# Second expert pass: the loads of activations and tables cut into pieces of two and four blocks

## Chip, cores and metric

The kernel runs on one core of a Trainium2 chip. The metric is device time in microseconds (us), the median over several executions.

## What is computed

The program is a first transformer block (windowed attention beside a state-space mixer, then an expert layer) followed by a second block of two layers. The change is in the expert layer of the first block, which is this part of the reference:

```
def peer_ffn(h, w_query, sub_keys, peer_u, peer_v):
    ...
        q = (hc @ w_query).astype(jnp.float32).reshape(PEER_CHUNK, PEER_HEADS, PEER_DK)
        ...
        v1, i1 = lax.top_k(s1, PEER_TOPK)
        v2, i2 = lax.top_k(s2, PEER_TOPK)
        ...
        sc, ci = lax.top_k(cand, PEER_TOPK)
        idx = ...
        g = jax.nn.softmax(sc, axis=-1)
        u_sel = peer_u[idx]
        act = jax.nn.gelu(jnp.einsum('chkd,cd->chk', u_sel, hc)...) * g
        v_sel = peer_v[idx]
        return jnp.einsum('chk,chkd->cd', act.astype(hc.dtype), v_sel)
```

Each of 512 tokens picks 8 x 16 of 16384 single-neuron experts. An expert's activation is the gelu of the token's dot product with a row of `peer_u`, times a gate; the output is the sum of the chosen rows of `peer_v` by these weights.

## The kernel before, in words

For three of the four groups of 128 tokens (384 tokens, `SD` = 384) the layer is computed densely. The 16384 experts lie in 128 blocks of 128. The text speaks of "expert n" for block n of the first pass and of "block n" for block n of the second.

- **First pass** (`experts_in`, driven by `phase_p1`): for each n a 512 KB tile `wraw` of `peer_u` is loaded by SyncE (SP), split by `split_sb` into a high part `whi` (ScalarE, ACT, L276) and a low part `wlo` (VectorE, DVE, L277), and multiplied by TensorE (PE) in 24 matmuls `pl` of 128x384 (L282 and L284 use `whi` and `wlo` of the weight). The gelu of the result goes to DRAM as `adram`, 12 KB of 8 blocks side by side in each partition.
- **Routing** (`route`): top-k, softmax and one-hot products that build the gate table `gdram`. Its DVE instructions (MATCH_REPLACE, MAX, MAX_INDEX, `cand`, `O`) are handed out between the experts of the first pass.
- **Sparse remainder** (`sparse_experts`): the fourth group of 128 tokens is done by gathering rows (GpSimd, POOL, L1133, with the index copy L1131 on DVE), dots on DVE in the first pass (L1142) and weighted sums `sacc` on DVE in the second (L1155).
- **Second pass** (`phase_p2`, 128 blocks): `fetch_ag(g)` loads for eight blocks the activations A (L1355, 1536 KB) and the gates G (L1356, 1536 KB) on SP's queue. `prep(n)` multiplies A by G for block n (L1376, DVE) and splits it into `ahl`: the high part on ACT (L276), the low part on DVE (L277). Then 18 matmuls `acc` of 128x512 use `ahl` and the split tile `whi`, `wlo` of a 512 KB `wraw` of `peer_v`.

Buffers: `wraw`, `whi`, `wlo` and `ahl` have three each, A and G two each. So `ahl` of block n+2 needs PE to have finished block n-1, the load of A for group g+1 needs the last `ahl` of group g-1, and the load of G for group g+2 needs the last multiply of group g. Every engine and every queue works in order. The order on each engine is set by a scheduler that runs the program against a simulated timeline when the kernel is built, so a change of a few DMAs can reorder other instructions. Program text:

```
if n % 8 == 0 and n < 120:
    self.fetch_ag(n // 8 + 1)
if n + 1 < 128:
    prep(n + 1)
ws.append((n, self.W.next(held=0)) + act.pop(n))
```

Of the kernel before, what the change touches and what calls it, by code (L numbers as in the profile page):

```python
# [204 lines left out]
class Stream:  # L205
# [46 lines left out]
    def next(self, held=0):  # L252

        n = self.n_used
        self._split(n + 1 + self.ahead - held)
        self.n_used += 1
        return self.got.pop(n)


class Kernel:  # L260
# [810 lines left out]
    def phase_p1(self):  # L1071
        nc, pp = self.nc, self.pp

        ring = self.p0.tile([128, 4, D], F32, name="ring", tag="xres")
        more = pp.tile([128, 2, D], F32, name="ring2")
        self.ring = [ring[:, j] for j in range(4)] + [more[:, j] for j in range(2)]
        self.sums = []
        self.hs = pp.tile([128, D], F32, name="hs")
        nc.gpsimd.dma_start(out=self.hs, in_=self.hdram)

        self.iota2 = pp.tile([128, 128, 2], F16, name="iota2")
        nc.vector.tensor_copy(self.iota2, self.iota[:, :, None].to_broadcast([128, 128, 2]))
        self.iota16 = pp.tile([128, 16, 16], BF16, name="iota16")
        nc.vector.tensor_copy(self.iota16, self.iota[:, :16, None].to_broadcast([128, 16, 16]))
        self.query()
        self.AG = {}
        first, rest, dense = self.route(0), chain(*(self.route(t) for t in range(1, TT))), self.experts_in()
        self.sparse = self.sparse_experts()

        have = 0.0  # L1090
        left = True
        for n, _ in enumerate(dense):
            have += 3.5
            while have > 0 and (d := next(first, None)) is not None:
                have -= d
            if have > 0:
                if n >= 12:
                    self.some(1.15)
                have -= 1.6
                while have > 0 and left:  # L1100
                    d = next(rest, None)
                    left = d is not None
                    have -= d or 0.0
                have = min(have, 0.0)
            if n >= 114 and not left and not self.AG:
                self.fetch_ag(0)
        for _ in chain(first, rest):
            pass

# [237 lines left out]
    def fetch_ag(self, g):  # L1347

        nc, pp = self.nc, self.pp
        A = pp.tile([128, 8 * SD + 16], F32, name="A2", tag="A2", bufs=2)  # L1350
        if g:
            self.hold = self.places(A, 8 * SD, 16)
        A = A[:, :8 * SD].rearrange("p (j t) -> p j t", j=8)
        G = pp.tile([128, SD // 32, 8, 32], F32, name="G2", tag="Gst", bufs=2)
        nc.sync.dma_start(out=A, in_=self.adram[g])  # L1355
        nc.sync.dma_start(out=G, in_=self.gdram[:, :, g * 8:g * 8 + 8].rearrange("t p i k -> p t i k"))  # L1356
        self.AG[g] = (A, G)

    def phase_p2(self):

        nc, pp = self.nc, self.pp
# [22 lines left out]

        if not self.AG:
            self.fetch_ag(0)
        prep(0)
        for n in range(128):
            if n % 8 == 0 and n < 120:
                self.fetch_ag(n // 8 + 1)  # L1390
            if n + 1 < 128:
                prep(n + 1)
            ws.append((n, self.W.next(held=0)) + act.pop(n))
            if n < 116:
                self.some(1.0)
            elif n == 116:
                for _ in self.sparse:
                    pass

                self.xres = self.p0.tile([128, TT, D], F32, name="xres")  # L1400
                nc.sync.dma_start(out=self.xres, in_=self.xdram)
            elif n == 120:
                x = self.xres[:, 0]
                v.tensor_tensor(x, x, self.sacc, op=OP.add)
                norm(0, None)
            if 128 - self.LAST <= n < 127:
                continue
            for t in range(1, TT):
                ts = slice((t - 1) * 128, t * 128)
                for m, w, hi, lo in ws:  # L1410
                    for h in range(2):
                        hs = slice(h * 512, h * 512 + 512)
                        self.mm3(acc[t][h], (hi[:, ts], lo[:, ts]), (w[0][:, hs], w[1][:, hs]), m == 0, m == 127)
                if n == 127:
                    for h in range(2):
                        x = self.xres[:, t, h * 512:h * 512 + 512]
                        v.tensor_tensor(x, x, acc[t][h], op=OP.add)
                        st = self.ln_stats(pp, self.xres[:, t], h, st if h else None)
                    norm(t, st)
            ws = []  # L1420
# [625 lines left out]
```

## Time and profile before

| | |
|---|---|
| median of 3 runs | 3328.93 us (3325.83 to 3332.78) |
| the profiled execution | 3332.02 us, span 3330.2 us, mean granted TensorE clock 0.983 |
| PE busy | 3169.8 us, 95% of the span |
| DVE busy | 2327.8 us, 70% |
| ACT busy | 1411.0 us, 42% |
| POOL busy | 909.1 us, 27% |
| first pass with routing | about 455 to 1152 us |
| second pass | about 1152 to 1705 us |

A row of the waits names an engine and line, what it waited for, the total, the count and the longest. A row of the timeline has start, duration, engine, line, operation, output, inputs, shapes; in brackets stands the idle time just before it and what ended it. PEclk is the granted TensorE clock as a share of full speed.

### The profile page before, as it was taken

To read this page: it belongs to the slowest core of one execution; us is meant where nothing else is said; L and a number is where in the kernel's file an instruction comes from. 1 tells how busy PE (TensorE), PEld (TensorE's weight loads), DVE (VectorE), ACT (ScalarE), POOL (GpSimd) and SP (SyncE) were. 2 spreads that over 40 slices of the span, in tenths; PEclk is the share of its full clock that TensorE was granted. 3 is DMA by queue.
4 is the path that set the end of the run, shared out by engine and by line. 5 is a ranking of instruction groups with operands and counts; after the bars stand their busy time and mean duration, and the time that the engine had idled before them with its cause. 6 is when DMAs were issued, how large, how long until landed. Compare 5 with 4: busy or idle time off the path is not lost.

```text
span 3330.2 us, 46422 instructions
## 1 busy us (share of the span) xinstructions
PE 3169.8 (95%) x17023; PEld 2704.6 (81%) x17023; DVE 2327.8 (70%) x4748; ACT 1411.0 (42%) x2396; POOL 909.1 (27%) x1114
## 2 busy tenths in 40 slices
PE   6888899999999899999999999999999999999997
PEld 5776689999999778777888778888888877888886
DVE  8899479999888678777867845555437774555534
ACT  4345434456555233333335733344314662434421
POOL 4342010333233323232222652311002365031101
PEclk9999899999999899999999999999999999999999
DMA  3464233889999989899742122222224112222222
GB/s 128 123 151 130 69 118 117 331 321 344 367 342 332 361 308 352 321 343 344 286 161 64 45 89 76 84 96 99 97 95 134 43 46 84 96 90 99 95 95 70
DMA packets 176164, 578.19 MB, mean 174 GB/s; under 512 B 19120, under 2 KB 52912, under 8 KB 169920
## 3 DMA queue, kind: packets, MB, share of 16 engines
q1 hardware_dynamic: 114576, 352.37, 30.8%
q0 software_dynamic: 43056, 165.69, 14.1%
q10 hardware_dynamic: 18304, 57.15, 4.4%
q8 instruction: 134, 2.20, 0.3%
q14 instruction: 94, 0.77, 0.1%
HBM read 511.72 MB, written 63.44 MB: 173 GB/s over the span
## 4 chain that ended last, share of the span: by engine, by line
PE 69%; DVE 14%; DMA 8%; issue 3%; POOL 3%; ACT 2%; SPq 0%; DVEq 0%; ACTq 0%; POOLq 0%
PE pl L284 11%; PE pl L282 11%; PE pl L283 11%; DMA wraw<-in_peer_v 4%; PE mm L282 2%; PE acc L282 2%; PE mm L283 2%; PE mm L284 2%; PE acc L284 2%; PE acc L283 2%; DMA A<-adram 2%; DVE wlo L277 2%; PE T L283 2%; PE T L284 2%; PE T L282 2%
## 5 line engine op out<-in xcount | busy, mean ns | idle before, releaser
L277 DVE TENSOR_TENSOR wlo<-wraw,whi 128x1024 fp32r<-128x1024 f32 x476 | 587.0, 1234 | 516.2 <-ACT whi L276 502.5
L276 ACT CAST whi<-wraw 128x1024 fp32r<-128x1024 f32 x507 | 529.4, 1048 | 807.7 <-PE pl L283 348.7
L282 PE MATMUL pl<-hhi,whi 128*128 128x384 f32 (+1 forms) x1128 | 390.1, 346 | 10.1 <-ACT whi L276 10.1
L284 PE MATMUL pl<-hhi,wlo 128*128 128x384 f32 (+1 forms) x1128 | 387.0, 345 | 10.2 <-DVE wlo L277 6.0
L283 PE MATMUL pl<-hlo,whi 128*128 128x384 f32 (+1 forms) x1128 | 388.3, 344 | 0.0
L282 PE MATMUL pl<-xThi,whi 128*128 128x512 f32 x944 | 370.4, 392 | 0.0
L284 PE MATMUL pl<-xThi,wlo 128*128 128x512 f32 x944 | 368.9, 391 | 0.0
L283 PE MATMUL pl<-xTlo,whi 128*128 128x512 f32 x944 | 368.3, 390 | 0.0
L283 PE MATMUL acc<-wlo,ahl 128*128 128x512 f32 x744 | 290.7, 394 | 0.0
L284 PE MATMUL acc<-whi,ahl 128*128 128x512 f32 x744 | 290.4, 393 | 0.0
L1133 POOL DMA_INDIRECT ring<-in_peer_v,A x128 | 160.1, 1251 | 382.2 <-DVE A L1131 276.9
L1133 POOL DMA_INDIRECT ring<-in_peer_r,A x123 | 158.3, 1287 | 329.6 <-DVE A L1131 304.1
L282 PE MATMUL acc<-whi,ahl 128*128 128x512 f32 x744 | 226.0, 396 | 10.5 <-ACT whi L276 10.5
L284 PEld LDWEIGHTS pl<-hhi,wlo 128*128 128x128 f32 x1128 | 213.3, 189 | 17.1 <-DVE wlo L277 13.1
L282 PEld LDWEIGHTS pl<-hhi,whi 128*128 128x128 f32 x1128 | 213.8, 190 | 15.3 <-ACT whi L276 11.3
L283 PEld LDWEIGHTS pl<-hlo,whi 128*128 128x128 f32 x1128 | 213.8, 190 | 3.7
L284 PEld LDWEIGHTS pl<-xThi,wlo 128*128 128x128 f32 x944 | 177.3, 188 | 39.2 <-issue 0.5
L283 PEld LDWEIGHTS pl<-xTlo,whi 128*128 128x128 f32 x944 | 177.2, 188 | 38.7 <-issue 1.0
L282 PEld LDWEIGHTS pl<-xThi,whi 128*128 128x128 f32 x944 | 177.3, 188 | 36.4 <-issue 0.5
L282 PEld LDWEIGHTS acc<-whi,ahl 128*128 128x128 f32 x744 | 139.1, 188 | 46.5 <-ACT whi L276 15.0
L2027 POOL TENSOR_TENSOR cv<-cv 128x512 f32<-128x512 f32 x44 | 57.0, 1296 | 431.0 <-ACT cv L2026 431.0
L283 PEld LDWEIGHTS acc<-wlo,ahl 128*128 128x128 f32 x744 | 139.9, 188 | 32.5
(715 smaller groups left out, 7349.4 us busy)
## 6 DMA issues: line engine op xcount, KB each, us to landing
wraw<-in_peer_u SPq DMA_DIRECT2D x128, 512.0 KB, 6.2
wraw<-in_peer_v SPq DMA_DIRECT2D x128, 512.0 KB, 8.4
wraw<-in_up SPq DMA_DIRECT2D x88, 512.0 KB, 3.4
adram<-A ACTq DMA_DIRECT2D x64, 384.0 KB, 6.7
A<-adram SPq DMA_DIRECT2D x16, 1536.0 KB, 7.4
gdram<-G ACTq DMA_DIRECT2D x12, 2048.0 KB, 10.8
G<-gdram SPq DMA_DIRECT2D x16, 1536.0 KB, 14.5
wraw<-in_down SPq DMA_DIRECT2D x44, 512.0 KB, 3.4
```

Of the source, the lines that this page charges most:

```text
L276: self.nc.scalar.copy(hi, src)
L277: (eng or self.nc.vector).tensor_tensor(lo, src, hi.bitcast(F32), op=OP.subtract)
L282: mm(out, l[0], r[0], start=start, stop=False)
L283: mm(out, l[0], r[1], start=False, stop=False)
L284: mm(out, l[1], r[0], start=False, stop=stop)
L1133: nc.gpsimd.indirect_dma_start(out=self.ring[n % R], out_offset=None, in_=src[n // 128], in_offset=bass.IndirectOffsetOnAxis(ap=ix, axis=0))
L2027: nc.gpsimd.tensor_tensor(ts[0], ts[0], ts[1], op=OP.mult)
```

## The change

`fetch_ag` becomes the start of a generator. A is loaded in four pieces of two blocks (384 KB, 128x768), G in two pieces of four blocks (768 KB, 128x12x128, where a contiguous run in DRAM is 512 bytes and was 1 KB). The first pieces are issued by the call, the others by `next` at every second block, and in the first pass at every further expert. The number of DMAs on SP's queue grows by four for each of 16 groups.

```diff
             if n >= 114 and not left and not self.AG:
                 self.fetch_ag(0)
+            if self.AG:
+                next(self.ag, None)
...
-        nc.sync.dma_start(out=A, in_=self.adram[g])
-        nc.sync.dma_start(out=G, in_=self.gdram[:, :, g * 8:g * 8 + 8].rearrange("t p i k -> p t i k"))
         self.AG[g] = (A, G)
+
+        def fetch():
+            for j in range(0, 8, 2):
+                nc.sync.dma_start(out=A[:, j:j + 2], in_=self.adram[g, :, j:j + 2])
+                if j % 4 == 0:
+                    nc.sync.dma_start(out=G[:, :, j:j + 4], in_=self.gdram[:, :, g * 8 + j:g * 8 + j + 4].rearrange("t p i k -> p t i k"))
+                yield
+        self.ag = fetch()
+        next(self.ag)
...
         if not self.AG:
             self.fetch_ag(0)
+        for _ in self.ag:
+            pass
         prep(0)
         for n in range(128):
             if n % 8 == 0 and n < 120:
                 self.fetch_ag(n // 8 + 1)
+            elif n % 2 == 0:
+                next(self.ag, None)
```

In the changed file the lines move: A is L1361, G L1363, the multiply L1385, the routing lines and `sparse_experts` stand two lines further down.

Three places show what the scheduler makes of it.

SP's queue in the second pass, from the load of A for blocks 48 to 55 (`A2_13140` before, `A2_13164` now) to the load of G for blocks 64 to 71. Before (`wraw` of blocks 41 to 43, G, then `wraw` of blocks 44 and 45):

```order
L1355 DMA A2_13140<-adram_84 128x3072
L226 DMA wraw_13024<-in_peer_v 128x1024
L226 DMA wraw_13055<-in_peer_v 128x1024
L226 DMA wraw_13086<-in_peer_v 128x1024
L1356 DMA G2_13645<-gdram_81 128x12x256
L226 DMA wraw_13117<-in_peer_v 128x1024
L226 DMA wraw_13152<-in_peer_v 128x1024
```

Now (one `wraw`, of block 41, between the third and the fourth piece, those of blocks 42 to 44 ahead of G, and block 45 behind it):

```order
L1361 DMA A2_13164<-adram_84 128x768 x3
L226 DMA wraw_13047<-in_peer_v 128x1024
L1361 DMA A2_13164<-adram_84 128x768
L226 DMA wraw_13078<-in_peer_v 128x1024
L226 DMA wraw_13110<-in_peer_v 128x1024
L226 DMA wraw_13141<-in_peer_v 128x1024
L1363 DMA G2_13677<-gdram_81 128x12x128 x2
L226 DMA wraw_13176<-in_peer_v 128x1024
L226 DMA wraw_13207<-in_peer_v 128x1024
```

The pieces are not spread over the eight blocks: three or four pieces of A stand in a row, both halves of G in a row, since a tile's first piece needs the whole buffer free. In the change as a whole, the first wraw behind G is that of blocks 21, 27, 37, 45, 51, 61, 69, 75, 85, 93 and 99 instead of 20, 29, 36, 44, 52 and so on, every eighth. A for blocks 32 to 39 stands ahead of the wraw of block 24, G behind that of block 26.

ACT in the second pass at blocks 43 to 48. Before, beginning with `ahl` of block 45, then `whi` of 44:

```order
L276 CAST ahl_13268<-A2_12888 128x384
L276 CAST whi_13210<-wraw_13117 128x1024
L276 CAST ahl_13299<-A2_12888 128x384
L276 CAST whi_13241<-wraw_13152 128x1024
L276 CAST ahl_13330<-A2_12888 128x384
L276 CAST whi_13272<-wraw_13183 128x1024
L276 CAST whi_13303<-wraw_13214 128x1024
```

Now, beginning with `ahl` of block 45 and `whi` of 44 as well (`ahl_13326` is block 46, `ahl_13358` block 47, `whi_13266` block 45):

```order
L276 CAST ahl_13295<-A2_12908 128x384
L276 CAST whi_13235<-wraw_13141 128x1024
L276 CAST ahl_13326<-A2_12908 128x384
L276 CAST ahl_13358<-A2_12908 128x384
L276 CAST whi_13266<-wraw_13176 128x1024
L276 CAST whi_13299<-wraw_13207 128x1024
L276 CAST whi_13330<-wraw_13239 128x1024
```

Before, `whi` of block n stands behind `ahl` of n+1; now, here, `ahl` of block 47 stands ahead of `whi` of block 45. Over the whole pass `ahl` of n+2 stands ahead of `whi` of n before at blocks 4, 20 and 116, and now at blocks 4, 21, 27, 45, 51, 69, 75, 93, 99 and 116. DVE has the low parts in the same order.

DVE in the first pass, the last rows ahead of `wlo` of expert 28 (`wlo_6496`). Before:

```order
L1131 COPY A_6648<-sidx_5519 128x1
L1142 ISA ring_4239,A_6648<-ring_4239,hs_4241 128x1024
L1142 ISA A_6648 128x1
L1327 TENSOR_TENSOR O_6164<-iota2_4243,T3_6050 128x1024
L277 TENSOR_TENSOR wlo_6496<-wraw_6321,whi_6495 128x1024
```

Now:

```order
L1133 COPY A_6648<-sidx_5519 128x1
L1144 ISA ring_4239,A_6648<-ring_4239,hs_4241 128x1024
L1144 ISA A_6648 128x1
L1248 MAX sc_9281<-cand_9274 128x8
L1334 TENSOR_TENSOR O_6164<-O_6164,g3_6051 128x2x256 x2
L1334 TENSOR_TENSOR O_6180<-O_6180,g3_6051 128x2x256 x2
L277 TENSOR_TENSOR wlo_6496<-wraw_6321,whi_6495 128x1024
```

Before, four rows stand between `wlo` of expert 27 and the first of these (a MAX and, for the other dot, an index copy and two ISA rows). Now 19 rows stand there: those four, both `O` builds (L1329 now), four `cand` rows and nine rows of small instructions. So between the two `wlo` the change has, beyond what stood there before, four `cand`, one `O` build, the four products of `O` (the last two rows ahead of `wlo`, each x2) and 13 small ones (MAX, MAX_INDEX, MATCH_REPLACE, `k`, `r3`). Up to `wlo` of expert 27 the same instructions have been issued in both.

## Rows read from the trace of the kernel before

**Rows 1.** Busy time by stretch: us, PE, PEld, DVE, ACT, POOL, PEclk, DMA share, GB/s.

```profile
600.00:700.00 100.00, 94.81 (x572) 92.35 (x572) 97.57 (x296) 49.59 (x69) 36.73 (x30) 0.98 0.92 334
...
1100.00:1152.00 52.00, 38.49 (x191) 37.04 (x192) 32.61 (x50) 11.17 (x16) 15.07 (x12) 0.84 1.00 365
1152.00:1705.00 553.00, 539.91 (x2335) 435.35 (x2334) 436.51 (x625) 194.70 (x264) 156.20 (x150) 1.00 0.84 312
```

**Rows 2.** What PE waited for, 1150 to 1710 us.

```profile
PE acc L282 <- ACT whi L276: 10.5, 10, 2.0
```

**Rows 3.** The chain of waits, 1430 to 1482 us: start, us, what.

```profile
1449.72 7.30 DMA A<-adram
...
1457.05 2.57 DVE A L1376 x6
...
1462.52 15.05 DMA wraw<-in_peer_v
...
1477.60 1.05 ACT whi L276
```

**Rows 4.** Timeline of PE, second pass: first matmuls after a wait.

```profile
1238.78 0.50 PE L282 MATMUL acc<-whi,ahl 128*128 128x512 f32 x1 [1.55 <-ACT whi L276]
...
1375.67 0.50 PE L282 MATMUL acc<-whi,ahl 128*128 128x512 f32 x1 [2.02 <-ACT whi L276]
...
1478.69 1.65 PE L282 MATMUL acc<-whi,ahl 128*128 128x512 f32 x6 [1.10 <-ACT whi L276]
```

**Rows 5.** Timeline of ACT, blocks 20 to 22 of the second pass.

```profile
1233.08 0.51 ACT L276 CAST ahl<-A 128x384 fp32r<-128x384 f32 x1 [3.60 <-PE acc L284]
1237.27 0.51 ACT L276 CAST ahl<-A 128x384 fp32r<-128x384 f32 x1 [3.68 <-PE acc L284]
1237.69 2.94 ACT L276 CAST whi<-wraw 128x1024 fp32r<-128x1024 f32 x3
```

**Rows 6.** Timeline of DVE and SP's queue, 1440 to 1485 us.

```profile
1457.05 3.84 DVE L1376 TENSOR_TENSOR A<-A,G 128x384 f32<-128x384 f32 x8 [1.64 <-DMA A<-adram]
...
1460.92 0.38 SPq L1356 DMA_DIRECT2D G<-gdram  x1
```

**Rows 7.** Timeline of DVE, experts 27 to 30 of the first pass.

```profile
656.69 1.22 DVE L277 TENSOR_TENSOR wlo<-wraw,whi 128x1024 fp32r<-128x1024 f32 x1
...
660.99 1.21 DVE L277 TENSOR_TENSOR wlo<-wraw,whi 128x1024 fp32r<-128x1024 f32 x1
...
662.33 0.67 DVE L1327 TENSOR_TENSOR O<-iota,T 128x1024 f16<-128x1024 f16 x1
...
662.99 0.75 DVE L1332 TENSOR_TENSOR O<-O,g 128x512 f16<-128x512 f16 x2
...
666.27 0.88 DVE L1234 TENSOR_TENSOR cand<-sall 128x128 f32<-128x128 f32 x4
```

**Rows 8.** Timeline of DVE, small routing instructions near 610 us.

```profile
609.62 0.73 DVE L1246 MAX8 sc<-cand 128x8 f32<-128x64 f32 x5
```

**Rows 9.** Timeline of PE: the first use of `wlo` of expert 28.

```profile
663.68 0.33 PE L284 MATMUL pl<-hhi,wlo 128*128 128x384 f32 x1
```

**Rows 10.** What PE waited for, 560 to 720 us.

```profile
PE pl L284 <- DVE wlo L277: 4.4, 4, 2.3
```

**Rows 11.** What PE waited for, 1080 to 1152 us.

```profile
PE pl L282 <- ACT whi L276: 8.5, 2, 6.4
PE pl L284 <- DVE A L1131: 4.2, 1, 4.2
```

**Rows 12.** Busy time by stretch, at the passage between the passes (columns as rows 1).

```profile
1120.00:1130.00 10.00, 5.80 (x20) 5.80 (x21) 9.10 (x13) 1.25 (x2) 5.24 (x4) 0.54 1.08 360
```

**Rows 13.** The chain of waits, 1086 to 1152 us.

```profile
1093.40 23.16 DMA G<-gdram
...
1117.06 3.37 DVE A L1376 x7
```

**Rows 14.** DMA queues, 1120 to 1126 us (pieces of 1 KB): packets, MB, share of 16 engines.

```profile
q1 hardware_dynamic: 2034, 2.07, 108.2%
```

**Rows 15.** DMA queues, 204 to 208 us (pieces of 512 bytes).

```profile
q10 hardware_dynamic: 272, 0.13, 11.4%
```

**Rows 16.** DMA rate in 40 slices, 1440 to 1475 us.

```profile
GB/s 392 410 407 417 234 28 0 126 403 70 169 403 183 267 323 393 435 370 389 431 407 421 435 393 412 417 407 408 400 389 391 330 284 301 355 391 392 406 398 410
```

## The prediction

> **What bounds the kernel now.** I read the busy times by stretch first. In the second pass (the last row of [rows 1]) PE is busy for 539.91 of 553 us at full granted clock and the DMA engines for 84%; DVE works 436.51 us and ACT 194.70, so both have room on the whole. PE sets the time there, and what a change can win is little: all of PE's waits for `whi` are 10.5 us, ten times [rows 2]. Next comes the chain of waits. One period of it reads [rows 3]: A is issued and lands 7.30 us later, DVE multiplies A by G, then G for a later group is issued [rows 6], the first `wraw` behind it on SP's queue takes 15.05 us, and ACT's `whi` comes only then. PE stands 1.10 us (the last of [rows 4]). Eight blocks, one in each group from block 44 to block 100, show this.
>
> The timeline of ACT shows the other two waits, at blocks 4 and 20 [rows 5]: two `ahl` in a row, each begins only after 3.6 us of waiting for PE, and `whi` comes behind the second at once, three of them in 2.94 us. So `whi` of block 20 was not late by its transfer; it stood behind `ahl` of block 22, which needed PE to have finished block 19. PE then had nothing to do for 1.55 us (the first of [rows 4]). This is a wait that the order alone makes. Taking 1.55 for block 4 as well, the eight others share 10.5 - 3.1 = 7.4 us, 0.93 each.
>
> In the first pass PE is nearly full too, but from 600 to 700 us DVE is busy for 97.57 of 100 us [rows 1], and PE waited four times for a `wlo`, 4.4 us [rows 10]. At the passage between the passes (1100 to 1152 us) PE works only 38.49 of 52 us with the DMA engines full; its waits [rows 11] and a clock of 0.54 between 1120 and 1130 us, the lower level (1.2 GHz) after the stop [rows 12], make up the loss. The chain there is two G loads, 23.16 us, then seven multiplies [rows 13].
>
> **The change, part by part.** It adds 64 DMA issues on SP, moves no byte more, cuts G's runs from 1 KB to 512 bytes, and through the scheduler moves work on ACT, DVE and SP.
>
> *Smaller G pieces.* In a stretch of 1 KB pieces 2034 packets took 108.2% of 16 engines for 6 us [rows 14]: 103.9 engine-us, 51 ns each. For 512 bytes it is 11.4% of 16 engines for 4 us over 272 packets [rows 15], 27 ns. A G load of 1536 packets of 1 KB becomes 3072: 1536 x 51 = 78 engine-us against 3072 x 27 = 83, over 16 engines +0.3 us; if a 512 byte packet cost two thirds of a large one (34 ns), +1.6. I take +0.5 us per G load, in the second pass inside the terms below.
>
> *More issues on SP.* One issue of G takes 0.38 us [rows 6]. Three more A issues delay the `wraw` behind them by about 1.1 us, one more G issue by 0.4. Queued behind are only `wraw` loads; ACT waits for them, and only the first behind G is ever late, so 0.4 us of it count below.
>
> *A forced wait at eight more blocks.* By the order, `whi` of block n now stands behind `ahl` of block n+2 at blocks 21, 27, 45, 51, 69, 75, 93 and 99 (block 4 stays, 20 goes). Nothing that is faster elsewhere can help: `ahl` of n+2 cannot start before PE ends block n-1, and PE has no `whi` for n. Price 1.55 us each, as at block 20: +12.4. The bounds: 0, if ACT reaches them early for a reason that I don't see, and 2.02, the longest wait of the kind with a transfer in it [rows 4].
>
> *The waits of the group go.* Behind G the first `wraw` is now that of 45 or 61 where it was 44 or 60; this gives PE a block, 553/128 = 4.3 us, more than the longest wait there. So -7.4, and -1.55 for block 20. Together the second pass stands at +3.4.
>
> *What is late next.* In every third group (27, 51, 75, 99) the first `wraw` behind G serves a block nearer to the release of A: four blocks after the last `ahl` that A waits for, where it was five. That costs 4.3 us of lead. Given back is this: the multiplies no longer begin when all of A is there; with two left after the last piece instead of eight, 6 x 3.84/8 = 2.9 us [rows 6]. So the `wraw` comes 0.93 + 4.3 - 2.9 + 0.4 (SP) = 2.7 us late where the order costs 1.55 anyway: about +1 each, +4 in all. Bounds: 0 (the order's wait covers it) and +2.9 each, if nothing is given back by the multiplies, +12.
>
> *First pass.* At expert 28 DVE gets to `wlo` later: ahead of it stand, by starts rather than by overlapping durations, four `cand` (0.8 us), one `O` build (0.6) and four products (1.3) [rows 7] and 13 small instructions of at most 0.73/5 = 0.15 [rows 8], 2.0: +4.7 us. In the trace `wlo` ends at 662.2 [rows 7] and PE first uses it at 663.68 [rows 9], 1.5 us later. PE loses 3.2 us. Later DVE has done that routing work already, but PE is full afterwards and cannot win it back. Bounds: 0, if the 1.5 us of slack grow because DVE's own waits for gathers move into the cover; +5, if the stop brings the lower clock again as at the passage.
>
> *The passage.* Two pairs of G loads, +0.5 us each, lie on the chain [rows 13]: +1 for the first pair, +1 for the second; against it, seven multiplies behind the last landing become three or four, -1.7, since half of G lands earlier. I take 0, from -3 (one `sacc` less is on the path too) to +3 (lower clock for longer).
>
> **Sum.** 3.4 + 4 + 3.2 + 0 = +10.6 us on the profiled execution of 3332.02 us: 3342.6. That execution was 3.1 us above the median of the runs shown (3328.93), so I forecast 3339.5 us. A measurement of this kernel tells some 0.2%, 6.7 us, from no change: below 3322.3 is faster, above 3335.6 slower.
>
> **Rivals.**
>
> *Slower by transfers* (0.10): the pieces stand together on SP, the burst of gathers that A releases comes into the smaller G packets, and the `wraw` of blocks 27, 51, 75 and 99 is late by its full 4.3 us: +12 instead of +4 there and +2 at the passage, 3350. For it: 15.05 us for one `wraw` behind G [rows 3]. Against: DVE's multiplies do start earlier.
>
> *No difference* (0.29): the pieces are not spread at all by the order, so the change hardly does what it says; the first pass keeps its slack (0) and the late `wraw` hide in the order's wait (0). Then +3.4 is left: 3332. For it: all terms are small, and DVE has room on the whole.
>
> *Faster, by a lead at the passage and in every group* (0.13): the multiplies run piece by piece, so G and all `wraw` behind it come up to 2.9 us earlier in every group, ACT is never behind, and the order's wait shrinks, because `ahl` of n+2 and `whi` of n both stand ready and only 1.05 us of `whi` [rows 3] is left partly beside PE's last matmuls. With x the order's wait per block and -3 at the passage, the sum is 8x - 8.95 - 3; it is below -6.7 once x is under 0.66 us. With x = 0.3 and no loss in the first pass: 3319. Against it [rows 4]: with three `whi` ready to go, PE still waited 1.55.
>
> *Many DMAs, each with its own start-up* (0.02). The trace shows rates near 400 GB/s while the queue holds only 512 KB loads and gathers [rows 16], so starts lie beside other transfers. If they did not, four more issues in each of 14 groups would lengthen the chain of rows 3 by at least an issue each and in the worst case by the wait of A itself, 7.30 us per group: over 100 us, 3430. Here the Trainium skill speaks against the change: its page "DMA: Bandwidth & Descriptors", in "Anatomy of one DMA", fits 2.0 us of fixed time to each DMA, and in "Rules for kernel authors" asks for at least 1 MiB per DMA; by it four more DMAs would be 8 us a group, +112 us as an estimate. That fit is for DMAs issued from GpSimd, these are issued from SP, and the 400 GB/s with 512 KB loads do not bear it out as a cost in series.
>
> **Chances.** The forecast itself, +7 to +15 us, has 0.46. Slower by over 0.2%: 0.46 + 0.10 + 0.02 = 0.58; within 0.2%: 0.29; faster: 0.13. The range reaches from the rival on the other side with x = 0.3 (3319, rounded to 3320) to the transfers' case with the first pass at its upper bound (3352); some 0.05 lie below and some 0.08 above.
>
> **What would show it.** Right: in the waits of the second pass, PE behind `whi` some nine or ten times for 17 to 20 us instead of 10.5, at the nine blocks named, ACT with two `ahl` before that `whi`, and no wait at 44, 52, 60 and so on; at blocks 27, 51, 75 and 99 more than 1.55 us. In the first pass a wait of PE for `wlo` of about 3 us near 664 us. Wrong: PE waiting for less than 0.7 us at blocks 45 or 69 (then the order does not bind), no new wait between 640 and 680 us, or a passage that is shorter by more than 3 us.

## The result and the profile after

The changed kernel takes 3364.32 us (median of 4 runs, 3362.39 to 3367.26), the kernel before 3328.19 us in the same session (4 runs, 3325.83 to 3332.78): 1.0101 times as long, interval 1.0089 to 1.0113. The ratios here and below are the record's own estimates; they can differ by up to 0.1% from the quotient of two medians (1.0109 here). The change costs 36 us where 10.6 was forecast, and the time lies above the range (3320 to 3352). The sign held; the size did not.

To find the stage that lost, I take the start of the same PE matmul in both profiled executions, counted from the first matmul of the routing's query, and write down by how much the lag grew in each stage. The table is worked out from the traces in this way, and holds all kernels of this study. All are held against the profiled execution of 3332.02 us.

```
lag gained per stage, us ("e24" expert 24 of the first pass, "b20" block 20 of the second)
               to e24  e24-e36 e36-e70 e70-e76 e76-e120 e120-b0  b0-b20  b20-end   rest    total
after           0.19    5.81    1.81    2.53   -1.62     4.81    -1.71    19.52    1.05    32.40
a_only          0.42    4.77    2.12    2.53   -1.62    -1.91    -1.71    14.99   -0.97    18.61
g_only          0.71   -0.13    0.12    0.01    0.00     5.63     0.36    11.82   -1.91    16.60
a2_once         0.10    0.63    0.02   -0.03    0.00    -1.58     0.01     2.23   -0.68     0.69
gt_once         0.37    0.03    0.00   -0.01    4.27    -7.17    -0.95    -0.32   -1.33    -5.13
a4_early        0.23    7.43    2.25    2.44   -1.62    -2.19     0.01     1.79    0.93    11.27
a4_late         0.48    0.01   -0.01    0.00    0.00     0.17    -1.72    17.23    0.49    16.66
a4_late_gact    0.65   -0.75    0.00    0.60    0.00    -1.17    -1.71    13.48    2.59    13.68
a4_nosacc       0.15   -0.01    0.00    0.01    0.00     0.33    -1.59    18.85   -1.26    16.48
gt3_first       0.07   -0.02    0.00    0.00    4.28    -9.32    -0.95     0.03   -1.75    -7.67
g_act4_gt3      0.54   -0.03    0.00    0.01    4.29    -7.98    -0.95    -9.63   -0.71   -14.45
g_act2_gt3      0.37    0.01    0.00    1.63    2.71    -9.51    -0.95    -9.63    0.00   -15.37
```

So the change loses 17.8 us in the second pass (the two columns from b0), 4.8 at the passage and 8.5 in the first pass from expert 24 to 120. Forecast were 7.4, 0 and 3.2.

The page of the changed kernel, busy times and DMA issues (KB each, median us from issue to landing):

```profile
PE 3178.9 (95%) x17023; PEld 2710.6 (81%) x17023; DVE 2331.7 (69%) x4748; ACT 1412.1 (42%) x2396; POOL 911.8 (27%) x1114
...
A<-adram SPq DMA_DIRECT2D x64, 384.0 KB, 6.6
G<-gdram SPq DMA_DIRECT2D x32, 768.0 KB, 13.0
```

No engine has much more to do than before: PE is busy for 9.1 us more (3169.8 before), part of it at a lower clock (below), DVE for 3.9. The rest of the 33 us is waiting.

**Second pass.** What PE waited for, 1150 to 1740 us (total, count, longest), against [rows 2]:

```profile
PE acc L282 <- ACT whi L276: 19.3, 9, 4.2
...
PE acc L283 <- DVE wlo L277: 4.8, 4, 1.7
```

The first row is what was forecast ("nine or ten times for 17 to 20 us"), the second is new: PE stands in the middle of a block, for `wlo`. The timeline of PE shows one of each kind, at blocks 69, 72 and 75:

```profile
1473.81 1.66 PE L282 MATMUL acc<-whi,ahl 128*128 128x512 f32 x6 [1.55 <-ACT whi L276]
...
1489.37 0.50 PE L283 MATMUL acc<-wlo,ahl 128*128 128x512 f32 x1 [1.38 <-DVE wlo L277]
...
1503.22 1.66 PE L282 MATMUL acc<-whi,ahl 128*128 128x512 f32 x6 [2.46 <-ACT whi L276]
```

At block 69 it is the order's wait, 1.55 us as at block 20 before [rows 4]. At block 75 it is longer, for the reason that ACT's timeline gives: `ahl` of block 77 goes first, and then `whi` still waits 0.82 us for its load.

```profile
1500.80 0.51 ACT L276 CAST ahl<-A 128x384 fp32r<-128x384 f32 x1 [3.68 <-PE acc L284]
1502.12 1.04 ACT L276 CAST whi<-wraw 128x1024 fp32r<-128x1024 f32 x1 [0.82 <-DMA wraw<-in_peer_v]
```

At block 72 the cause stands in DVE's timeline: ACT had written `whi` of block 72 at 1484.76 (1483.71 and 1.05), but DVE stood for 2.99 us at a `sacc` whose gathered row had not come, and `wlo` of block 72 (the second row) is queued behind it, four multiplies, an `ahl` and another `sacc`.

```profile
1483.36 1.28 DVE L1157 SCALAR_TENSOR_TENSOR sacc<-ring,dots,sacc 128x1024 f32<-128x1024 f32 x1 [2.99 <-DMA ring<-in_peer_v,A]
...
1488.10 1.22 DVE L277 TENSOR_TENSOR wlo<-wraw,whi 128x1024 fp32r<-128x1024 f32 x1
```

Over the pass, what DVE waited for says it in one row, after:

```profile
DVE sacc L1157 <- DMA ring<-in_peer_v,A: 19.9, 12, 3.0
```

and before:

```profile
DVE sacc L1155 <- DMA ring<-in_peer_v,A: 0.4, 1, 0.4
```

At blocks 24, 48 and 96 it reads the same: DVE stands 2.50, 2.47 and 2.69 us at a `sacc`, and PE then waits 0.73, 0.94 and 1.71 us for the `wlo` behind it. At all four blocks DVE stood longer than PE waited.

From the same starts of matmuls, block by block: the eight forced blocks 21, 27, 45, 51, 69, 75, 93 and 99 lose 1.61, 2.75, 1.6, 4.38, 1.61, 2.62, 1.6 and 2.46 us, 18.6 together, and the waits that go (block 20 and every eighth from 44) give time back. Steps with no counterpart in the forecast are of two kinds. Four are the waits for `wlo`, 1.05, 1.27, 1.66 and 2.02 us, 6.0 together (at 25, 49, 73 and 97; a wait in the middle of a block shows in the next one's start, so that of block 72 stands at 73). Two are the clock. After 2.58 us without work ahead of block 27 and 4.22 us ahead of block 51, PE's first six matmuls take 2.15 and 2.12 us (1.66 at block 69), and each of these blocks lasts 5.84 us to the start of the next, where 4.12 was the rule before,

```profile
1286.19 2.15 PE L282 MATMUL acc<-whi,ahl 128*128 128x512 f32 x6 [2.58 <-ACT whi L276]
...
1395.38 2.12 PE L282 MATMUL acc<-whi,ahl 128*128 128x512 f32 x6 [4.22 <-ACT whi L276]
```

and the stretches behind them (columns as [rows 1]) have a granted clock of 0.71 and 0.66 in the mean, between the two levels of 1.2 and 2.4 GHz, where the 5 us before each had 1.00:

```profile
1285.00:1290.00 5.00, 3.81 (x11) 2.99 (x12) 4.59 (x4) 3.14 (x3) 0.00 (x0) 0.71 0.52 192
...
1395.00:1400.00 5.00, 4.62 (x13) 3.67 (x14) 3.68 (x3) 2.43 (x3) 0.00 (x0) 0.66 0.46 125
```

At block 28 the step is 1.72 us. At block 52 the clock's loss is hidden: the old wait of 2.02 us is gone there, which gives 2.10 back in g_act4_gt3 (below), but here only 0.45, so 1.65 was lost. With 2.10 at block 52 the waits that go give 10.1 back, and the clock takes 3.4.

18.6 - 10.1 + 6.0 + 3.4 = 17.9, the 17.8 of the table but for rounding.

**First pass.** What PE waited for, 560 to 720 us, against [rows 10]:

```profile
PE pl L284 <- DVE wlo L277: 4.6, 4, 2.3
PE pl L282 <- ACT whi L276: 3.4, 3, 1.4
```

The forecast wait for `wlo` of expert 28 is not there: the row on `wlo` is as before. New are waits for ACT. The lag steps are 1.65 us at expert 26, 4.11 at 29, 3.91 at 73. ACT's timeline around expert 28:

```profile
661.72 1.05 ACT L276 CAST whi<-wraw 128x1024 fp32r<-128x1024 f32 x1
662.79 1.28 ACT L1258 ACT_TABLE_LOAD   x1
...
664.41 1.28 ACT L1217 ACT_TABLE_LOAD   x1
...
666.60 1.05 ACT L276 CAST whi<-wraw 128x1024 fp32r<-128x1024 f32 x1
```

and PE's:

```profile
667.70 0.44 PE L282 MATMUL pl<-hhi,whi 128*128 128x384 f32 x1 [1.25 <-ACT whi L276]
...
669.56 0.69 PE L282 MATMUL pl<-hhi,whi 128*128 128x384 f32 x1 [0.76 <-ACT A L1217]
...
671.20 0.67 PE L284 MATMUL pl<-hhi,wlo 128*128 128x384 f32 x1
```

The first of ACT's rows is `whi` of expert 28, the last that of 29; between them stands an exponential of the routing with two table loads (2 x 1.28 us), which stood behind `whi` of 29 and 30 before. And PE's own order has changed too. The order of PE in the changed kernel (`whi_6495` and `wlo_6496` are expert 28, 6564 is 29, 6616 is 30; before, the 24 matmuls of 28 stood in one piece):

```
L282 MATMUL pl_6622<-hhi_3809,whi_6495 128x384
L283 MATMUL pl_6622<-hlo_3810,whi_6495 128x384
L282 MATMUL pl_6692<-hhi_3809,whi_6564 128x384
L283 MATMUL pl_6692<-hlo_3810,whi_6564 128x384
...
L282 MATMUL pl_6745<-hhi_3809,whi_6616 128x384
L283 MATMUL pl_6745<-hlo_3810,whi_6616 128x384
...
L284 MATMUL pl_6622<-hhi_3809,wlo_6496 128x384
```

So PE waits at 667.70 for `whi` of 29 and at 669.56 for a result buffer that ACT's L1217 frees, and takes `wlo` of 28 only at 671.20, though that was ready at 668.39. DVE's part was forecast well:

```profile
657.79 1.22 DVE L277 TENSOR_TENSOR wlo<-wraw,whi 128x1024 fp32r<-128x1024 f32 x1
...
667.16 1.23 DVE L277 TENSOR_TENSOR wlo<-wraw,whi 128x1024 fp32r<-128x1024 f32 x1
```

9.37 us between the two `wlo`, where [rows 7] have 4.30: 5.1 more, 4.7 forecast. At expert 73 ACT stands 2.65 us at a gelu, by the row until a gather is done, and DVE and PE stand with it (DVE 5.08 us, for that gelu); a gelu stood so before as well, 2.21 us at 863.21:

```profile
871.77 0.49 ACT L1217 ACTIVATE A<-pl 128x384 f32<-128x384 f32 x1 [2.65 <-DMA ring<-in_peer_r,A]
```

**The passage.** PE's two long waits for `whi` are 16.8 us, against 8.5; the wait for L1131 of [rows 11] (L1133 now) has shrunk from 4.2 to 1.0:

```profile
PE pl L282 <- ACT whi L276: 16.8, 2, 8.4
```

SP's queue of the changed kernel has G's eight pieces in two runs of four; while they are issued, for 19.33 and 10.89 us (2.0 us of the second in a wait), no `wraw` can be:

```profile
1100.31 19.33 SPq L1363 DMA_DIRECT2D G<-gdram  x4
...
1124.20 10.89 SPq L1363 DMA_DIRECT2D G<-gdram  x4
1135.18 11.29 SPq L226 DMA_DIRECT2D wraw<-in_peer_u  x2
```

and before:

```profile
1092.97 5.91 SPq L1356 DMA_DIRECT2D G<-gdram  x2
1100.10 10.65 SPq L226 DMA_DIRECT2D wraw<-in_peer_u  x3
...
1124.17 1.60 SPq L226 DMA_DIRECT2D wraw<-in_peer_u  x2
```

Expert 120 starts at 1098.7 before and at 1108.2 after, so 9.5 us of each difference are older. The chain of waits of the changed kernel goes from those last two issues to the last `whi` of the pass:

```profile
1135.18 18.30 DMA wraw<-in_peer_u
1153.56 1.05 ACT whi L276
```

Before, that `whi` ran behind ACT's gelu, not behind its load:

```profile
1138.98 0.50 ACT A L1215
...
1139.92 1.05 ACT whi L276
```

From 1139.92 to 1153.56 it is 13.6 us, 4.2 more than the 9.5: a load that had time to spare is late now.

### The profile page after: what moved, and what is told of

It reads as the page before. It is cut to its first block, busy times and chain, and to the rows that moved or that the text cites. A ratio compares the mean times of both kernels' runs of the same rounds, so it can differ in the third digit from the quotient of the medians.

```text
span 3363.4 us, 46520 instructions
## 1 busy us (share of the span) xinstructions
PE 3178.9 (95%) x17023; PEld 2710.6 (81%) x17023; DVE 2331.7 (69%) x4748; ACT 1412.1 (42%) x2396; POOL 911.8 (27%) x1114
## 4 chain that ended last, share of the span: by engine, by line
PE 64%; DVE 14%; issue 9%; DMA 5%; POOL 5%; ACT 2%; DVEq 0%; SPq 0%; POOLq 0%; ACTq 0%
PE pl L282 9%; PE pl L283 9%; PE pl L284 9%; PE acc L283 4%; PE acc L284 4%; PE acc L282 4%; PE mm L282 2%; PE mm L283 2%; PE mm L284 2%; POOL ring L1135 2%; DVE wlo L277 2%; PE T L283 2%; PE T L284 2%; PE T L282 2%; DMA ring<-in_peer_v,A 1%
## 5 line engine op out<-in xcount | busy, mean ns | idle before, releaser
L284 PE MATMUL acc<-whi,ahl 128*128 128x512 f32 x744 | 292.1, 395 | 0.0
L282 PE MATMUL acc<-whi,ahl 128*128 128x512 f32 x744 | 238.9, 397 | 19.3 <-ACT whi L276 19.3
L1157 DVE SCALAR_TENSOR_TENSOR sacc<-ring,dots,sacc 128x1024 f32<-128x1024 f32 x127 | 162.9, 1283 | 21.1 <-DMA ring<-in_peer_v,A 20.1
```

Of the source, the lines that this page charges most:

```text
L282: mm(out, l[0], r[0], start=start, stop=False)
L284: mm(out, l[1], r[0], start=False, stop=stop)
L1157: v.scalar_tensor_tensor(self.sacc, r, w, self.sacc, op0=OP.mult, op1=OP.add)
```

## The experiments

Theories. **Order**: what costs is the order that the scheduler makes of A's four pieces. **Runs**: what costs is G's 512-byte runs in DRAM, with the queue behind them. **Count**: what costs is the number of DMAs. The quoted text under each was written before it ran. Each kernel ran in three rounds beside the kernel before on the same chip.

**a_only**: A in four pieces, G whole.

```diff
-                if j % 4 == 0:
-                    nc.sync.dma_start(out=G[:, :, j:j + 4], ...)
+                if j == 0:
+                    nc.sync.dma_start(out=G, ...)
```

> A in four pieces of two blocks as in the change, G whole as before (one load of 1 KB runs). The scheduler gives this kernel the changed kernel's order: in the first pass DVE's order parts from the old one at the same instruction as the changed kernel's, and in the second pass whi of block n stands behind ahl of n+2 at the same ten blocks (4, 21, 27, 45, 51, 69, 75, 93, 99, 116). Theory 'order' (the four A pieces move instructions on ACT and DVE, and that is the cost): first pass +8 us, second pass +17 us as in the changed kernel (measured there between first and last block: +17.8), passage 0 to +3, in all 3352 to 3358 us. Theory 'queue' (G's 512-byte runs fill SP's queue; in the changed kernel the second half of G took 5 us to issue, and the loads behind it come late): the second pass loses only the eight forced waits against the eight old ones, +4, so 3338 to 3343 us.

Measured: 3349.5 us, ratio 1.0054 (1.0036 to 1.0072): a little below the range of theory 'order', above that of 'queue'.

**g_only**: A whole, G in two halves.

```diff
-                nc.sync.dma_start(out=A[:, j:j + 2], in_=self.adram[g, :, j:j + 2])
+                if j == 0:
+                    nc.sync.dma_start(out=A, in_=self.adram[g])
```

> G in two halves of four blocks (512-byte runs) as in the change, A whole as before. The order on ACT and DVE in the second pass is that of before (whi behind ahl of n+2 at blocks 4, 20 and 116 only). Theory 'order': little, up to +5 us at the passage, 3328 to 3334 us, and PE's waits for whi in the second pass stay at 10 to 13 us. Theory 'queue': the wraw behind G comes later by the time that SP needs to issue the second half (about 5 us), at eight to eleven groups, 3345 to 3380 us.

Measured: 3348.72 us, ratio 1.0047 (1.0029 to 1.0066), in the range of 'queue' and far above that of 'order'. So each half of the change costs about as much as the other, and they lose in different places. A alone brings the changed order on all engines and the loss in the first pass (7.8 us from expert 24 to 120) and the second (13.3), none at the passage. G alone leaves the order nearly as it was, loses nothing in the first pass, 5.6 us at the passage and 12.2 in the second. What PE waited for in the second pass, in a_only,

```profile
PE acc L282 <- ACT whi L276: 14.6, 9, 1.9
PE acc L283 <- DVE wlo L277: 5.6, 6, 1.6
```

and in g_only:

```profile
PE acc L282 <- ACT whi L276: 19.4, 11, 2.4
```

In g_only the old waits behind G [rows 2] have grown from 10.5 to 19.4 us. From the starts and landings of DMAs, as a mean over the groups from block 44 to 100, G takes 16.3 us from its first issue to its last landing where it took 14.9, and the `wraw` behind it lands after 17.7 instead of 16.2. In the first pass and at the passage the two costs add up in the changed kernel; in the second they would be 25.5 and are 17.8. The waits of the changed kernel show where the cost of G is hidden: of the eleven blocks whose `wraw` is the first behind G, PE waits longer than the order's 1.55 us at 27, 51, 75 and 99 alone, 1.55 at 21, 45, 69 and 93, and not at all at 37, 61 and 85. Blocks 27, 51, 75 and 99 lose 3.05 us on average in the changed kernel, but 1.87 in a_only and 2.17 in a4_late (below), which have the same order and G whole. So most of what they lose above 1.6 needs G in halves.

**a2_once** (A in two pieces back to back) and **gt_once** (G in two pieces of six table rows, whose runs stay 1 KB long): more DMAs, neither the changed order nor short runs.

```diff
-        nc.sync.dma_start(out=A, in_=self.adram[g])
+        for j in range(0, 8, 4):
+            nc.sync.dma_start(out=A[:, j:j + 4], in_=self.adram[g, :, j:j + 4])
```

> A in two pieces of four blocks, issued one after the other, G whole. The scheduler leaves the order nearly as before: same forced waits (4, 20, 116), the first pass the same up to its end. Theory 'order': cutting A costs nothing by itself, 3325 to 3332 us. Rival, 'each DMA has its price' (a start-up in series with the transfer): 14 more A loads of some 2 us each on the chain from A to the late wraw, +15 to +30 us, 3343 to 3358.

```diff
-        nc.sync.dma_start(out=G, in_=self.gdram[:, :, g * 8:g * 8 + 8].rearrange("t p i k -> p t i k"))
+        for t in range(0, 12, 6):
+            nc.sync.dma_start(out=G[:, t:t + 6], in_=self.gdram[t:t + 6, :, g * 8:g * 8 + 8].rearrange("t p i k -> p t i k"))
```

> G in two DMAs as in the change, but cut by the rows of the gate table (six of twelve each), so that a run stays 1 KB; A whole. Forced waits at 20 and 116 only. Theory 'run length' (the G halves of the change cost because of 3072 packets of 512 bytes instead of 1536 of 1 KB): second pass 0 to +2 us, first G half at the passage earlier, 3322 to 3332 us. Rival 'number of DMAs' (a second DMA has its own price in SP's queue): second pass +8 to +12 us as with G in halves by blocks, 3336 to 3344 us.

Measured: 3334.76 us, ratio 1.0011 (1.0001 to 1.0022), and 3325.81 us, ratio 0.998 (0.9971 to 0.999). The first lies just above the range of its theory and below that of its rival, the second in the range of its theory. Neither costs more than the 0.2% that a measurement can tell; gt_once is rather faster. gt_once and g_only have the same 32 loads of 768 KB; they differ in the length of the runs. The page of gt_once,

```profile
G<-gdram SPq DMA_DIRECT2D x32, 768.0 KB, 13.2
```

and of g_only:

```profile
G<-gdram SPq DMA_DIRECT2D x32, 768.0 KB, 14.3
```

So **count** falls for 16 more DMAs (the change has 64 more, and no run here adds so many with the order kept), and **runs** stands in the second pass. The packets agree: from 1180 to 1620 us those of 512 bytes took 31.8 ns in the mean in the changed kernel, those of 1 KB 49.4 before, and 3072 x 31.8 - 1536 x 49.4 over 16 engines is 1.4 us for each G load. Not all of the 21.7 us between gt_once and g_only come from the runs. In gt_once the forced wait of block 4 is gone from the order (1.6 us); and at the passage, where it gains 2.9 us (4.27 - 7.17), it issues its first G at 1057 us, when the first half of the table rows has been written, and not at 1093 us.

**a4_early** and **a4_late**: A in four pieces for the first two groups only, and for the others only (`k = 2 if g < 2 else 8`, here as it stands in a4_late).

```diff
-        nc.sync.dma_start(out=A, in_=self.adram[g])
+        k = 2 if g > 1 else 8
+        for j in range(0, 8, k):
+            nc.sync.dma_start(out=A[:, j:j + k], in_=self.adram[g, :, j:j + k])
```

> A in four pieces only for the two loads in the first pass, the rest as before. The scheduler gives the first pass the changed order and leaves the second pass in the old one (4, 20, 116). Theory 'order': first pass +8 to +9 us, passage -2, second pass 0: 3334 to 3340 us. Rival 'the pieces collide with the first pass's loads' (not the order but the two extra loads cost): the loss sits near the two loads of A at some 630 to 690 us alone, +2 us, 3329 to 3333 us.

> A in four pieces only for the fourteen groups that are loaded in the second pass; the two loads of A in the first pass and all of G as before. The scheduler leaves the first pass in the old order and gives the second pass the changed order (forced waits at the ten blocks). Theory 'order': first pass 0, passage 0, second pass +13 us as with A in pieces throughout (there +13.3 by stage): 3340 to 3346 us. Rival 'the first pass sets off the rest' (what is late in the second pass is late because of how the first pass ended): second pass +4 or less, 3328 to 3336 us.

Measured: 3338.01 us, ratio 1.0013 (1.0002 to 1.0024), and 3343.32 us, ratio 1.003 (1.0019 to 1.0041). By the table a4_early loses nearly all in the first pass (10.5 us from expert 24 to 120) and a4_late only in the second (15.5); the second pass does not need a late first pass. a4_early alone does not separate the order from the transfer, though: the first load of A stands right there, as four issues in place of one, and part of the loss lies where the rival puts it. The first row is a4_early's, the second that of the kernel before:

```profile
631.41 2.00 SPq L1357 DMA_DIRECT2D A<-adram  x4
...
631.52 0.33 SPq L1355 DMA_DIRECT2D A<-adram  x1
```

Two readings speak for the order. The weight loads behind these pieces (experts 25 to 27) land at 645.8, 649.3 and 652.1 us, and before at 645.5, 650.2 and 652.9, so the pieces made them no more than 0.3 us later. And a2_once has two pieces of A at the same place and the old order in the first pass, and loses 0.63 us from expert 24 to 36 where a4_early loses 7.43. Four pieces with the old order were not run. Medians say less than the profiled executions here, 6 and 11 us.

**a4_late_gact**: a4_late, with G of groups 4 to 15 issued by ACT, so that no `wraw` stands behind G on a queue. If transfers made the forced waits, they would go; if the order does, they stay.

```diff
-        nc.sync.dma_start(out=G, ...)
+        (nc.scalar if g > 3 else nc.sync).dma_start(out=G, ...)
```

> As the run with A in four pieces in the second pass alone (there the second pass lost 17 us), but the G loads of the second pass are issued by ACT, so no wraw stands behind G in SP's queue. The order still puts whi of n behind ahl of n+2 at blocks 4, 21, 27, 45, 51, 69, 75, 93, 99 and 116. Theory 'the order forces the wait': PE stands 1.55 us at each of 21, 27, 45, 51, 69, 75, 93 and 99, the longer ones at 27, 51, 75 and 99 shrink to that, and the waits for wlo at 25, 49, 73 and 97 stay: second pass +6 to +10 us against before, 3336 to 3342 us in all. Rival 'only the transfers make the waits': with G out of the way they go as they did in the run with G issued by ACT, second pass -8 to -10, 3318 to 3325 us.

Measured: 3343.2 us, ratio 1.0038 (1.0027 to 1.005), slightly above what the order theory gave and far above the rival. PE's waits in the second pass:

```profile
PE acc L282 <- ACT whi L276: 18.9, 13, 1.7
...
PE acc L283 <- DVE wlo L277: 1.2, 4, 0.3
```

No wait is longer than 1.7 us, and by the starts of matmuls blocks 21, 45, 69 and 93 lose 1.6, and 27, 51, 75 and 99 all 1.71. That is the order's price alone at these blocks, as taken from block 20. What blocks 27, 51, 75 and 99 lose above it in the changed kernel (1.0, 2.7, 0.9 and 0.75 us) goes with a late `wraw`: with whole G loads on SP's queue 0, 1.1, 0.2 and 0.5 are left (a4_late), and without a G ahead on the queue it is gone.

The waits for `wlo` at 25, 49, 73 and 97, which were to stay, have become waits for `whi` at 24, 48, 72 and 96 (1.28, 1.03, 0.93 and 1.71 us, four of the 13). G's issue now stands on ACT: it needs the last multiply of an older group, DVE comes to that late because of a `sacc`, and ACT's `whi` is queued behind the issue. At block 24 DVE had stood 2.79 us at a `sacc`, its multiplies ended at 1252.31, and ACT had been idle for 3.8 us:

```profile
1252.34 0.37 ACTq L1358 DMA_DIRECT2D G<-gdram  x1
1252.80 1.05 ACT L276 CAST whi<-wraw 128x1024 fp32r<-128x1024 f32 x1 [3.83 <-DVE ahl L277]
```

**a4_nosacc**: a4_late without the sums of the gathered rows in the second pass, all but the first (this part of the computation is left out), so that DVE has nothing to stand at.

```diff
-                v.scalar_tensor_tensor(self.sacc, r, w, self.sacc, op0=OP.mult, op1=OP.add)
+                pass
```

> A in four pieces in the second pass alone, as in the run that lost 17 us there, but the weighted sums sacc of the second pass are left out on DVE (all but the first; the gathers stay), so that no wlo stands behind a sum that waits for its gathered row. The order keeps the forced waits at 21, 27, 45, 51, 69, 75, 93 and 99. Theory: the waits of PE for wlo at blocks 25, 49, 73 and 97 (1.2 to 1.8 us each, and the longer waits at 28 and 51 beside them) come from DVE standing at sacc for a gather: they go, the forced waits stay, second pass +8 to +12 us against before instead of +17. Rival: they come from DVE's whole load or from late wraw: they stay, +15 to +19.

Measured: 3347.86 us, ratio 1.0051 (1.0034 to 1.0067). The place was right, the total wrong. PE's waits in a4_late,

```profile
PE acc L282 <- ACT whi L276: 16.2, 10, 2.7
PE acc L283 <- DVE wlo L277: 4.7, 5, 1.5
```

and in a4_nosacc, where no row for `wlo` is left:

```profile
PE acc L282 <- ACT whi L276: 21.0, 10, 3.4
```

So the waits for `wlo` in the middle of a block go with `sacc`. The run takes away the work of the sums too (1.28 us each), so by itself it does not exclude the rival's "whole load" of DVE; the timeline of the changed kernel above does, where DVE stood idle at a `sacc` for longer than PE waited. But blocks 27, 51, 75 and 99 now lose 3.1 to 3.6 us, the clock falls again behind 27, 51 and 75 (0.66, 0.50 and 0.66 in the mean of 5 us), and what was won is lost again. In the trace the `wraw` behind G land later: 17.8 us after G's issue at block 27 and 18.5 at block 75, where a4_late has 14.1 and 14.9. That the gathers, which no sum holds back any more, are the reason was not tested.

**gt3_first**, **g_act4_gt3**, **g_act2_gt3**: what would help the kernel before. The first cuts G of the first four groups into three pieces of four table rows (1 KB runs). The second does this too, and issues G of the later groups from ACT; in the third the limits are two groups instead of four (`g < 2`, `g > 1`).

```diff
-        nc.sync.dma_start(out=G, in_=self.gdram[:, :, g * 8:g * 8 + 8].rearrange("t p i k -> p t i k"))
+        k = 4 if g < 4 else 12
+        for t in range(0, 12, k):
+            (nc.scalar if g > 3 else nc.sync).dma_start(out=G[:, t:t + k], in_=self.gdram[t:t + k, :, g * 8:g * 8 + 8].rearrange("t p i k -> p t i k"))
```

> The kernel before, but the G loads of the first four groups in three pieces by the rows of the gate table (four of its twelve rows each, 1 KB runs), so that two of three pieces of the first group need not wait for the last table write; the scheduler issues two pieces of the first group seven experts earlier, and drops the forced wait at block 4. If the passage is bound by the late G loads (two loads, 23 us on the chain, PE idle for some 16 us): the passage gets shorter by 3 to 8 us, 3318 to 3326 us. If it is bound by the DMA engines, which are full there whatever comes first: 3326 to 3331 us.

> The first four G loads in three pieces by the rows of the gate table as in the run before (3326.6 us), and all later G loads issued by ACT instead of SP, so that the wraw behind G is no longer behind it in one queue. If the eight waits of the second pass (7.4 us) come from standing behind G in SP's queue: they go, 3316 to 3322 us. Rival: the DMA engines are full then anyway, the wraw shares them with G and lands as late, and ACT loses 0.4 us and more per issue: 3325 to 3335 us.

> As the run with the later G loads issued by ACT and the first ones in three pieces (3313 us), but the third and fourth G load are issued by ACT as well, whole, and only the first two by SP in pieces. If what is left of the loss at the passage comes from wraw standing behind the second pair of G loads in SP's queue: another 3 to 6 us, 3307 to 3311 us. Rival: the DMA engines are the bound at the passage and packets of two queues share them, so nothing moves, 3311 to 3317 us; or ACT stands at the issue of G and delays whi, 3317 to 3325 us.

Measured: 3326.63 us, ratio 0.9987 (0.9977 to 0.9996); **3313.23 us, ratio 0.9934 (0.9917 to 0.9951)**; 3317.13 us, ratio 0.9958 (0.9941 to 0.9974). The first lies where its two theories meet (its passage is 5.0 us shorter, -9.32 + 4.28), the second a little below its range. The second beats both kernels. Its second pass gains 9.6 us more than gt3_first, since the eight waits for a `wraw` behind G are gone. PE's waits there:

```profile
PE acc L282 <- ACT whi L276: 1.5, 1, 1.5
```

Its DMA issues from 1150 to 1690 us (KB each, median us to landing):

```profile
wraw<-in_peer_v SPq DMA_DIRECT2D x124, 512.0 KB, 7.6
...
G<-gdram ACTq DMA_DIRECT2D x12, 1536.0 KB, 18.1
```

G lands 18.1 us after its issue where it took 14.5 before, and nobody waits for it; the `wraw` come in 7.6 instead of 8.4. The third kernel, which moves two more G loads to ACT, shows the same 9.63 us in this stage and no more: the 3 to 6 us that were expected on top did not come.

## Why the prediction was wrong in size

The sum was 10.6 us and the trace shows 32.4. By its own steps:

- *A forced wait at eight more blocks*: right. 1.55 us was forecast, and 1.6 was found at blocks 21, 45, 69 and 93, and 1.71 where a4_late_gact takes the transfers out of the others.
- *The waits of the group go*: right. 8.95 us was forecast for them with block 20, 10.1 found, which takes 1.1 off the sum.
- *What is late next*: right blocks, a little small. Blocks 27, 51, 75 and 99 were to lose 2.55 each and lose 3.05 on average, +2.0 in all. That the size comes so near is in part luck: the term was built on the shorter lead, with 0.4 us for G's second issue, and a_only and a4_late, which have the shorter lead and G whole, lose only 1.87 and 2.17 there.
- **Not in the sum at all: waits for `wlo` behind `sacc`, +6.0 us, and the clock behind the long waits at blocks 27 and 51, +3.4.** "DVE has room on the whole" was the step that failed. DVE has room and works in order: it now stands at sums whose gathered rows are late (19.9 us in 12 waits against 0.4), and `wlo` stands behind them. I followed what ACT has queued behind a late input, and did not do the same for DVE. DVE's timeline and a4_nosacc show that these waits come from the sums; why the gathers come later was not tried. The clock was priced in for the first pass and the passage, but not here.
- **The term of the first pass was mis-sized: 3.2 us forecast, 8.5 measured**, and the wait was another one. The delay of `wlo` 28 was right (5.1 against 4.7), but PE does not wait for it: I had compared DVE's order alone. On ACT an exponential with two table loads went ahead of `whi` of 29, a conversion of the routing ahead of `whi` at expert 25, and on PE the first matmuls of 29 and 30 went ahead of most of 28; expert 73 is a third place with a wait for a gather. a_only and a4_early have this loss with G whole; that it is the order and not the pieces themselves rests on the landings and on a2_once.
- **The passage: 0 forecast, +4.8 measured**, and g_only has it too (+5.6), a_only and a4_late don't. The price of a G load was the step: 0.5 us taken between 0.3 and 1.6, 1.4 measured in the second pass (16.3 - 14.9, and the same from the packets), near the upper bound. Of the two rows, the one with 1 KB packets came from a stretch with the queue full, the one with 512 bytes from a quiet stretch; "34 ns if two thirds" was the better guide. And the term followed the chain from G to the multiplies, while the chain that now binds goes from the issue of G over the last `wraw` of the first pass, which had time to spare before.
- The rest: +0.2 in the forced blocks, 1.2 outside these stages. 10.6 - 1.1 + 2.0 + 6.0 + 3.4 + 5.3 + 4.8 + 0.2 + 1.2 = 32.4.

Of the rivals, *slower by transfers* named the right places (27, 51, 75, 99 and the passage), but at the four blocks 6.0 us above the order's 1.55 were found, nearer to the forecast's 4 than to its 12. *No difference* was right that the pieces are not spread and wrong that this is harmless. *Faster, by a lead* needed an order's wait under 0.66 us; it is 1.55 or more at all eight blocks. *Many DMAs, each with its own start-up* fell: by the trace a2_once, with one more A load in every group, loses 0.7 us and gt_once, with 16 more G loads, gains 5.1. The Trainium skill ("DMA: Bandwidth & Descriptors", "Anatomy of one DMA") fits 2.0 us of fixed time to each DMA. As a cost in series that would be, as an estimate from this figure, 32 us in either, and no run here shows it.

## What to carry to other kernels

Where a scheduler sets the order, cutting one load into four can reorder every engine, where the load stands and far from it; compare the order of every engine, not only of the one that looks full, and for each instruction that waits for something new ask what is queued behind it. Cut a load along the axis that keeps its runs in DRAM long. And where an urgent load stands in line behind a large one that nobody waits for, give the large one another queue: that, with the first G loads in three pieces, took 0.66% off here, where the finer cut added 1%. Look then at what the engine that issues it stands for: in a4_late_gact ACT stood for the buffer of G, and an urgent conversion was late behind that issue.

## What was not expected of the hardware

- With the number and size of the loads equal, halving the runs from 1 KB to 512 bytes made the second pass 13.5 us longer (b0 to the end: 12.2 in g_only, -1.3 in gt_once; up to 1.6 of it is a forced wait). From 1180 to 1620 us a packet of 512 bytes took 31.8 ns in the changed kernel and one of 1 KB 49.4 before: not half, but 64%.
- The issue of a DMA on SP is not always short. One issue of G took 0.38 us [rows 6], but in the changed kernel two halves in a row behind four pieces of A and three `wraw` took 5.69 us (0.38 and 5.26), and the `wraw` behind them could only be issued then:

```profile
1486.55 5.69 SPq L1363 DMA_DIRECT2D G<-gdram  x2
1492.34 13.76 SPq L226 DMA_DIRECT2D wraw<-in_peer_v  x5
```

  It is not a matter of halves: before, a pair of whole G loads at the passage took 5.91 us, and the issue of the `wraw` behind the one G of [rows 6] 5.37 us. So the time seems to go with what is outstanding on the queue; no run varied that alone.
- A wait in the second pass can cost more than its length: behind the 2.58 us ahead of block 27 and the 4.22 us ahead of block 51 the granted clock was 0.71 and 0.66 in the mean of 5 us, and 1.7 us more were lost each time. I had priced these waits at full clock. The length of the wait alone does not tell which: 2.46 us at block 75 here and 3.17 at block 99 in a4_nosacc left the clock at 1.00, and 1.94 us at block 75 in a_only brought it to 0.66.
- Two loads on the queues of two engines seem to share the transfers: with G on ACT's queue it landed 3.6 us later (18.1 against 14.5), and the 512 KB loads on SP's 0.8 us earlier, and the waits for them were gone.
